# A hybrid attention and state-space block: the state-space loads in another order, and its prelude in buffers of its own

## The chip, the cores and the metric

The kernel runs on one core of one Trainium2 chip. TensorE (PE), VectorE (DVE), ScalarE (ACT), GpSimd (POOL) and SyncE (SP) each work through a list of instructions of their own, in order; DMA transfers are issued from queues, nearly all of them from SP's. The metric is the device time of one execution in microseconds (us).

## The reference, cut to what matters

One layer over 512 tokens of width 1024, float32. One projection feeds three token mixers: DSA (attention over keys that an indexer picks), NSA (compressed, selected and windowed attention) and SSD (a state-space mixer, 32 heads in 4 groups, 4 chunks of 128 tokens). Their outputs are projected, gated, summed, projected again, and a feed-forward network follows. The change concerns the SSD mixer:

```python
dtc = softplus(dt + dt_bias)                 # a step per token and head
a = -exp(a_log)
a_cum = cumsum(dtc * a, axis=2)              # along the 128 tokens of a chunk
lmat = exp(where(tril, a_cum_i - a_cum_j, -inf))
cb = einsum('bcign,bcjgn->bcijg', cm, bm)
y_diag = einsum('bcijg,bcijgh,bcjgh,bcjghp->bcighp', cb, lmat, dtc, xs)
states = einsum('bcjgn,bcjgh,bcjghp->bcghpn', bm, exp(a_cum[:, :, -1:] - a_cum) * dtc, xs)
h_in = scan over chunks: h = h * exp(a_cum[:, :, -1]) + states
y_off = einsum('bcign,bcghpn,bcigh->bcighp', cm, h_in, exp(a_cum))
y = rms_norm((y_diag + y_off + xs * d_skip) * silu(z), norm_g)
```

## The kernel before, in words

Two streams of work are written out together. The **filler** is the stream of projections: matmuls into PSUM tiles `pj`, three per product (high and low halves of both operands: lines 359 to 361), with weight blocks loaded by SP (`wraw`), split by ACT (`whi`, line 158) and DVE (`wlo`, line 159). The **main** stream runs the DSA indexer (a top-k by repeated `max` and `match_replace` on DVE, lines 766 to 774), the SSD prelude, the DSA attention of 16 units, the SSD mixer of 16 units, and the NSA attention. Generators yield amounts of work, and a scheduler with a timeline of its own then fixes each engine's order; the chip runs that order as it stands.

PSUM has two buffers for `pj`, two for `sc`, two for `pT`, one each for `pv` and `pF`. A pool tag `gt` with two SBUF buffers (`TG` is 2) holds, in turn, outputs that go to memory. The z projections use it:

```python
def cbz(t, p):
    zo = gp.tile([128, 512], F32, name="zo", tag="gt", bufs=TG)
    act.activation(zo, p, AF.Tanh, scale=0.5)
    dve.scalar_tensor_tensor(zo, zo, 1.0, p, op0=ALU.add, op1=ALU.mult)
    nc.sync.dma_start(zs_d[...], zo)
```

A `pj` buffer is free again when DVE has done the second of these (line 619). The two tiles `pre` of the SSD prelude come from the same tag: from the prelude's first operation until its last tile has gone to `ac_d` in memory, they are the two `gt` buffers.

The SSD mixer works on 16 units (a group and a chunk each; units 0, 1, 2, ... alternate between two groups). A unit loads `E` (the row of `a_cum` spread over partitions, 512 KB), `xs` and `zs` (256 KB each) and `bcx` (B transposed, B and C, three loads of 64 KB), all on SP's queue. `stage2` makes the product of C and B on PE (line 1139, "cb"), a mask on POOL (line 1142), eight exponentials on ACT (1145) and a product on DVE (1152), all in `E`; `stage3` makes the unit's output from `E` and `xt` with eight matmuls on PE (line 1180, "py"), the state's matmuls before them (1163, 1170), then two DVE operations and a transpose (1191). Each of the four tiles has two buffers, and the loads of unit i+2 are written ahead of `stage3` of unit i, which is the last to read the buffers that they go to.

Of the kernel before, what the change touches and what calls it, by code (L numbers as in the profile page):

```python
# [7 lines left out]
F32 = mybir.dt.float32  # L8
# [26 lines left out]
R0, R1, R2, R3 = 1000.0, 1.5, 2.5, 0.5  # L35


def build_kernel(ctx, tc, A, out):
    nc = tc.nc
# [14 lines left out]
    def popen(name, side="left", space=None, bufs=1):  # L54
        kw = dict(name=name, bufs=bufs, side=side)
        if space is not None:
            kw["space"] = space
            kw.pop("side")
        cm = tc.tile_pool(**kw)
        p = cm.__enter__()  # L60
        open_pools[name] = cm
        return p

    def pclose(name):
        open_pools.pop(name).__exit__(None, None, None)
# [8 lines left out]
    xs_d = scratch("xs_d", [S, 2048])  # L74
    bt_d = scratch("bt_d", [S, 512])
# [13 lines left out]
    def ps(tag, shape, dt=F32, bufs=2):  # L89
        if tag == XT[0]:  # L90
            XT[1] += 1
            if XT[1] % 3 == 0:
                tag = "pF"
        return psp.tile(shape, dt, tag=tag, name=tag, bufs=PSB[tag])
# [7 lines left out]
    gp = popen("gt")  # L102
# [757 lines left out]
    def pipeline(units, ratio):  # L860
        prev = None
        for u in units + [None]:
            if u is not None:
                if u.load is not None:
                    yield from u.load()
                u.prep()
                yield from a1(u, ratio)
            if prev is not None:
                yield from b1(prev, ratio)
            if u is not None:  # L870
                a2(u)
            prev = u
# [182 lines left out]

    def ssd_prelude():
        n = [128, 128]
        pre = [gp.tile([128, 4, 128], F32, name="pre", tag="gt", bufs=TG) for _ in range(2)]
        t = {k: pre[i // 4][:, i % 4] for i, k in enumerate("xaebsuvt")}
        tri1 = t["t"]  # L1060
        pool.memset(tri1, 1.0)
# [25 lines left out]
        dta = t["e"]  # L1087
        dve.scalar_tensor_tensor(dt3(dta), dt3(dt), -1.0, bc(av[:, None, :], [128, 4, 32]), op0=ALU.mult, op1=ALU.mult)
        yield 700.0
        ones = t["u"]  # L1090
        pool.memset(ones, 1.0)
        p = ps("pT", [128, 512])
# [9 lines left out]
        dve.tensor_scalar(sv["ea"], sv["ea"], 0.5, None, op0=ALU.mult)  # L1102
        dve.tensor_scalar(dskip, dskip, 0.5, None, op0=ALU.mult)
        yield 700.0
        p = ps("pT", [128, 512])
        pe.transpose(p[:, 0:128], sv["acm"], ident)
        at_ = t["s"]
        dve.tensor_copy(at_, p[:, 0:128])
        nc.sync.dma_start(ac_d, at_)
        return sv  # L1110

    def ssd(sv, ratio):
        sp = popen("ssd", side="right")
# [4 lines left out]
        def stage1(g, c):  # L1118
            u = U()
            u.g, u.c = g, c  # L1120
            rows = slice(c * 128, c * 128 + 128)
            cols = slice(g * 512, g * 512 + 512)
            u.E = sp.tile([128, 8, 128], F32, name="E", bufs=2)
            nc.sync.dma_start(u.E, bcast_rows(ac_d, c * 32 + g * 8, 8))
            u.xs = sp.tile([128, 512], F32, name="xs", bufs=2)
            nc.sync.dma_start(u.xs, xs_d[rows, cols])
            u.zs = sp.tile([128, 512], F32, name="zs", bufs=2)
            nc.sync.dma_start(u.zs, zs_d[rows, cols])
            u.b = sp.tile([128, 3, 128], F32, name="bcx", bufs=2)
            nc.sync.dma_start(u.b[:, 0], bt_d[rows, g * 128:g * 128 + 128])  # L1130
            nc.sync.dma_start(u.b[:, 1], BC_d[g * 128:g * 128 + 128, rows])
            nc.sync.dma_start(u.b[:, 2], BC_d[512 + g * 128:512 + g * 128 + 128, rows])
            return u

        def stage2(u):
            g, c = u.g, u.c
# [65 lines left out]
        def need(i):  # L1202
            if i < 16:
                g, c = order[i]
                if c == 0:
                    yield f"x{g}"
                    yield f"z{g}"
                us.append(stage1(g, c))
        us = []
        yield from need(0)  # L1210
        yield from need(1)
        yield from stage2(us[0])
        for i in range(16):
            yield from need(i + 2)
            if i + 1 < 16:
                yield from stage2(us[i + 1])
            if TR:
                TR.pop()()
                yield ratio * 436
            yield from stage3(us[i])  # L1220
        TR.pop()()
        yield ratio * 436
        sst = sp.tile([128, 4], F32, name="sst")
# [12 lines left out]
    def bcast_rows(t, r0, n):  # L1236
        a = t[r0:r0 + n, :]
        return bass.AP(tensor=a.tensor, offset=a.offset, ap=[[0, 128]] + [list(e) for e in a.ap])
# [240 lines left out]
    def main():  # L1479
        nonlocal at  # L1480
        HI[0] = 0
        yield from dsa_index(mk)
        yield "dq"
        yield "nkv"
        sv = yield from ssd_prelude()
        at = popen("att", side="right")
        HI[0] = HM
        yield from pipeline(dsa_units(), R1)
        pclose("att")
        pclose("mask")  # L1490
        yield from ssd(sv, R3)
        XT[0] = "pT"
        yield "nq"
        at = popen("att", side="right")
        yield from pipeline(nsa_units(R2), R2)
        done.add("nsa")
        yield "c1"
        pclose("att")
        pclose("kv")
# [60 lines left out]
```

## Time and profile before

| | us |
|---|---|
| median of three runs | 1436.81 (1435.62 to 1438.63) |
| the profiled execution, its own time | 1434.21 |
| span from the first to the last instruction in it | 1432.5 |
| PE busy in it | 1364.9 |
| from the first cb (404.5) to the end of the SSD's last transposes (about 591) | 187 |

The profiled execution stands 2.6 us below the median of the runs. Its own time is 1.7 us more than its span. PE's busy time counts matmuls that overlap once; what PE lacks to the span is idle time.

### The profile page before, as it was taken

The numbers are of one execution on the slowest core, as the hardware profiler recorded it, in microseconds if no ns is written. First come the engines' busy times: TensorE is split into PE (matmuls) and PEld (weight loads), VectorE is DVE, ScalarE is ACT, GpSimd is POOL, SyncE is SP. The second block draws the span as 40 slices with busy tenths as digits, with TensorE's granted clock in tenths as the row PEclk, the third lists the DMA queues.
The fourth block names the chain that finished last, engine by engine and source line by source line (L and its number), as shares of the span: only waits on it lengthen the run. The fifth ranks groups of instructions, "written<-read, shape, count | busy, mean of one in ns | idle before, by whom it ended". The sixth has DMA issues, their size and how long they took to land.

```text
span 1432.5 us, 19782 instructions
## 1 busy us (share of the span) xinstructions
PE 1364.9 (95%) x6736; PEld 1121.9 (78%) x6736; DVE 1089.1 (76%) x1944; ACT 722.5 (50%) x1442; POOL 482.4 (34%) x342
## 2 busy tenths in 40 slices
PE   6989799999999989999999999999799999999988
PEld 5878688888887767888888777787589888888866
DVE  4599966898977555488568897888655797979796
ACT  5545236667665675555555555545324444444442
POOL 5455211101056676111013524424000342526265
PEclk9999899999999999999999999999899999999999
DMA  6336464453586688843337743424555232331401
GB/s 202 81 96 139 126 205 126 136 133 103 139 229 200 202 230 218 229 141 107 89 94 208 207 129 100 117 65 131 178 184 172 79 118 89 106 115 53 136 4 59
DMA packets 232098, 195.93 MB, mean 137 GB/s; under 512 B 17200, under 2 KB 183484, under 8 KB 231996
## 3 DMA queue, kind: packets, MB, share of 16 engines
q1 hardware_dynamic: 226524, 183.12, 44.3%
q0 software_dynamic: 4608, 8.39, 2.2%
q10 hardware_dynamic: 864, 3.15, 0.6%
q8 instruction: 53, 0.87, 0.3%
q14 instruction: 49, 0.40, 0.1%
HBM read 157.85 MB, written 36.77 MB: 136 GB/s over the span
## 4 chain that ended last, share of the span: by engine, by line
PE 70%; DVE 14%; DMA 7%; issue 4%; ACT 3%; POOL 2%; SPq 1%; DVEq 0%; POOLq 0%; ACTq 0%
PE pj L359 16%; PE pj L360 16%; PE pj L361 15%; PE sc L359 3%; PE sc L361 3%; PE sc L360 3%; PE pT L831 2%; DVE wlo L159 2%; PE sc L796 2%; PE sc L795 2%; PE pv L844 2%; PE pv L843 1%; DMA gld<-g_d 1%; DVE mask L766 1%; DMA E<-ac_d 1%
## 5 line engine op out<-in xcount | busy, mean ns | idle before, releaser
L158 ACT ACTIVATE whi<-wraw 128x1024 fp32r<-128x1024 f32 (+3 forms) x180 | 173.2, 971 | 176.3 <-PE pj L360 115.7
L159 DVE TENSOR_TENSOR wlo<-wraw,whi 128x1024 fp32r<-128x1024 f32 (+1 forms) x156 | 192.9, 1238 | 60.3 <-ACT whi L158 59.2
L359 PE MATMUL pj<-hTh,whi 128*128 128x512 f32 x384 | 154.9, 403 | 0.4 <-DVE cacc L726 0.4
L361 PE MATMUL pj<-hTh,wlo 128*128 128x512 f32 x384 | 153.6, 400 | 0.0
L360 PE MATMUL pj<-hTl,whi 128*128 128x512 f32 x384 | 153.3, 399 | 0.0
L359 PE MATMUL pj<-whi,hTh 128*128 128x512 f32 (+2 forms) x352 | 141.6, 404 | 8.3 <-DVE stk L429 3.1
L804 ACT ACTIVATE p<-p,nb,rs 128x256 f32<-128x256 f32 (+3 forms) x192 | 123.2, 645 | 52.0 <-DVE nb L802 52.0
L360 PE MATMUL pj<-wlo,hTh 128*128 128x512 f32 (+2 forms) x352 | 139.6, 397 | 0.1
L361 PE MATMUL pj<-whi,hTl 128*128 128x512 f32 (+2 forms) x352 | 138.3, 393 | 0.0
L159 DVE TENSOR_TENSOR wlo<-qd,whi 128x1024 fp32r<-128x1024 f32 x56 | 101.3, 1815 | 25.6 <-ACT whi L158 25.6
L359 PE MATMUL pj<-yh,whi 128*128 128x512 f32 x256 | 103.6, 409 | 9.8 <-ACT yh L709 8.2
L815 POOL TENSOR_TENSOR p<-p,rc 128x256 f32<-128x256 f32 (+3 forms) x48 | 38.2, 796 | 220.7 <-DVE rc L810 67.1
L158 ACT ACTIVATE whi<-qd 128x1024 fp32r<-128x1024 f32 x56 | 58.9, 1055 | 87.6 <-PE sc L361 38.9
L360 PE MATMUL pj<-yl,whi 128*128 128x512 f32 x256 | 102.6, 401 | 0.3 <-DVE yl L710 0.3
L361 PE MATMUL pj<-yh,wlo 128*128 128x512 f32 x256 | 102.3, 400 | 0.0
L359 PE MATMUL sc<-whi,fh 128*128 128x512 f32 x224 | 88.9, 397 | 8.2 <-DVE u2acc L1460 4.8
L360 PE MATMUL pj<-h2l,whi 128*128 128x512 f32 (+1 forms) x256 | 96.3, 376 | 0.0
L361 PE MATMUL pj<-h2h,wlo 128*128 128x512 f32 (+1 forms) x256 | 96.2, 376 | 0.0
L359 PE MATMUL pj<-h2h,whi 128*128 128x512 f32 (+1 forms) x256 | 96.1, 376 | 0.0
L360 PE MATMUL sc<-wlo,fh 128*128 128x512 f32 x224 | 88.6, 396 | 0.0
L361 PE MATMUL sc<-whi,fo 128*128 128x512 f32 x224 | 88.3, 395 | 0.0
L359 PEld LDWEIGHTS pj<-whi,hTh 128*128 128x128 f32 x352 | 68.2, 194 | 22.4 <-issue 6.6
(349 smaller groups left out, 3476.3 us busy)
## 6 DMA issues: line engine op xcount, KB each, us to landing
wraw<-in_w_in_dram SPq DMA_DIRECT2D x84, 512.0 KB, 4.4
wraw<-in_w_ff_dram SPq DMA_DIRECT2D x32, 512.0 KB, 4.3
qd<-in_w_ff_dram SPq DMA_DIRECT2D x32, 512.0 KB, 4.7
gld<-g_d SPq DMA_DIRECT2D x48, 256.0 KB, 3.2
q_d<-qev SPq DMA_DIRECT2D x128, 64.0 KB, 2.7
qu<-q_d POOLq DMA_DIRECT2D x32, 256.0 KB, 3.6
E<-ac_d SPq DMA_DIRECT2D x16, 512.0 KB, 4.9
wraw<-in_w_br_ssd_dram SPq DMA_DIRECT2D x16, 512.0 KB, 4.0
```

Source lines behind the costliest of these rows:

```text
L158: act.activation(hi[:, :m], r[:, :m], AF.Copy)
L159: (pool if i < NP else dve).tensor_tensor(lo[:, :m], r[:, :m], f(hi[:, :m]), op=ALU.subtract)
L359: pe.matmul(o, lh, rh, start=first, stop=False)
L360: pe.matmul(o, lh, rl, start=False, stop=False)
L361: pe.matmul(o, ll, rh, start=False, stop=last)
L766: dve.scalar_tensor_tensor(wk, r[:, :n], iwt[:, b, h:h + 1], caus[:, 384 - 128 * b:] if h == 0 else wk, op0=ALU.mult, op1=ALU.add)
L795: pe.matmul(s_[:, h % w, :n], u.q[:, h], kh[:, :n], start=True, stop=False)
L796: pe.matmul(s_[:, h % w, :n], u.q[:, h], kl[:, :n], start=False, stop=True)
L804: act.activation(u.p[h][:, :n], u.p[h][:, :n], AF.Exp, bias=u.nb[:, h:h + 1], scale=rs8[:, u.b, u.h0 + h:u.h0 + h + 1], accum_out=u.sm[:, ...
L815: pool.tensor_tensor(u.p[h][:, :n], u.p[h][:, :n], bc(rc[:, h:h + 1], [128, n]), op=ALU.mult)
L831: pe.transpose(pt[:, h], u.p[h][:, kb * 128:kb * 128 + 128], ident)
L844: pe.matmul(o, vk, pl0, start=False, stop=en)
```

## The change

The prelude gets a pool of its own, `pre`, on the side of SBUF where the indexer's tiles lay, closed after the DSA attention. Its last two parts (the matmuls with what reads them, and the transpose with the store to `ac_d`) become generators of their own and run as the `load` of units 5 and 7 of the DSA attention. In the SSD mixer `bcx` and `xs` have three buffers, the loads of `bcx` stand first, `E` of unit i+2 is loaded after `stage3` of unit i, and `zs` of unit i+1 just before its `stage2`.

```diff
--- before.py
+++ after.py
@@ -1055,7 +1055,8 @@
 
     def ssd_prelude():
         n = [128, 128]
-        pre = [gp.tile([128, 4, 128], F32, name="pre", tag="gt", bufs=TG) for _ in range(2)]
+        pp_ = popen("pre", side="right")
+        pre = [pp_.tile([128, 4, 128], F32, name="pre", bufs=2) for _ in range(2)]
         t = {k: pre[i // 4][:, i % 4] for i, k in enumerate("xaebsuvt")}
         tri1 = t["t"]
         pool.memset(tri1, 1.0)
@@ -1087,6 +1088,9 @@
         dta = t["e"]
         dve.scalar_tensor_tensor(dt3(dta), dt3(dt), -1.0, bc(av[:, None, :], [128, 4, 32]), op0=ALU.mult, op1=ALU.mult)
         yield 700.0
+        return sv, t, tri1, dta
+
+    def ssd_prelude2(sv, t, tri1, dta):
         ones = t["u"]
         pool.memset(ones, 1.0)
         p = ps("pT", [128, 512])
@@ -1102,12 +1106,14 @@
         dve.tensor_scalar(sv["ea"], sv["ea"], 0.5, None, op0=ALU.mult)
         dve.tensor_scalar(dskip, dskip, 0.5, None, op0=ALU.mult)
         yield 700.0
+
+    def ssd_prelude3(sv, t):
         p = ps("pT", [128, 512])
         pe.transpose(p[:, 0:128], sv["acm"], ident)
         at_ = t["s"]
         dve.tensor_copy(at_, p[:, 0:128])
         nc.sync.dma_start(ac_d, at_)
-        return sv
+        yield 100.0
 
     def ssd(sv, ratio):
         sp = popen("ssd", side="right")
@@ -1120,17 +1126,21 @@
             u.g, u.c = g, c
             rows = slice(c * 128, c * 128 + 128)
             cols = slice(g * 512, g * 512 + 512)
-            u.E = sp.tile([128, 8, 128], F32, name="E", bufs=2)
-            nc.sync.dma_start(u.E, bcast_rows(ac_d, c * 32 + g * 8, 8))
-            u.xs = sp.tile([128, 512], F32, name="xs", bufs=2)
-            nc.sync.dma_start(u.xs, xs_d[rows, cols])
-            u.zs = sp.tile([128, 512], F32, name="zs", bufs=2)
-            nc.sync.dma_start(u.zs, zs_d[rows, cols])
-            u.b = sp.tile([128, 3, 128], F32, name="bcx", bufs=2)
-            nc.sync.dma_start(u.b[:, 0], bt_d[rows, g * 128:g * 128 + 128])
+            u.b = sp.tile([128, 3, 128], F32, name="bcx", bufs=3)
             nc.sync.dma_start(u.b[:, 1], BC_d[g * 128:g * 128 + 128, rows])
             nc.sync.dma_start(u.b[:, 2], BC_d[512 + g * 128:512 + g * 128 + 128, rows])
+            nc.sync.dma_start(u.b[:, 0], bt_d[rows, g * 128:g * 128 + 128])
+            u.xs = sp.tile([128, 512], F32, name="xs", bufs=3)
+            nc.sync.dma_start(u.xs, xs_d[rows, cols])
             return u
+
+        def load_E(u):
+            u.E = sp.tile([128, 8, 128], F32, name="E", bufs=2)
+            nc.sync.dma_start(u.E, bcast_rows(ac_d, u.c * 32 + u.g * 8, 8))
+
+        def load_z(u):
+            u.zs = sp.tile([128, 512], F32, name="zs", bufs=2)
+            nc.sync.dma_start(u.zs, zs_d[u.c * 128:u.c * 128 + 128, u.g * 512:u.g * 512 + 512])
 
         def stage2(u):
             g, c = u.g, u.c
@@ -1208,16 +1218,22 @@
                 us.append(stage1(g, c))
         us = []
         yield from need(0)
+        load_E(us[0])
         yield from need(1)
+        load_E(us[1])
+        load_z(us[0])
         yield from stage2(us[0])
         for i in range(16):
             yield from need(i + 2)
             if i + 1 < 16:
+                load_z(us[i + 1])
                 yield from stage2(us[i + 1])
             if TR:
                 TR.pop()()
                 yield ratio * 436
             yield from stage3(us[i])
+            if i + 2 < 16:
+                load_E(us[i + 2])
         TR.pop()()
         yield ratio * 436
         sst = sp.tile([128, 4], F32, name="sst")
@@ -1482,11 +1498,15 @@
         yield from dsa_index(mk)
         yield "dq"
         yield "nkv"
-        sv = yield from ssd_prelude()
+        sv, *rest = yield from ssd_prelude()
         at = popen("att", side="right")
         HI[0] = HM
-        yield from pipeline(dsa_units(), R1)
+        us = dsa_units()
+        us[5].load = lambda: ssd_prelude2(sv, *rest)
+        us[7].load = lambda: ssd_prelude3(sv, rest[0])
+        yield from pipeline(us, R1)
         pclose("att")
+        pclose("pre")
         pclose("mask")
         yield from ssd(sv, R3)
         XT[0] = "pT"
```

The scheduler then orders every engine anew. Up to the prelude's matmuls PE's order is the same; behind them, as far as the last projections of the branches, pieces of attention, mixer and filler stand at other places against each other. Three places follow, with the rows of each engine's order.

PE, before, in the middle of the first z projection (`pj`), where the prelude's two cumulative sums (lines 1093, 1094) and its transpose (1106) stand:

```order
L360 MATMUL pj<-wlo,hTh 128x512
L361 MATMUL pj<-whi,hTl 128x512
L1093 MATMUL pT<-pre 128x128
L1094 MATMUL pT<-pre 128x128
L1106 MATMUL pT<-ident,sv_acm 128x128
L359 MATMUL pj<-whi,hTh 128x512
L360 MATMUL pj<-wlo,hTh 128x512
```

PE, after: at the old place there are only matmuls of `pj`; the two sums (now lines 1097 and 1098) stand in the DSA attention, between the value matmuls of a unit (843, 844) and the next unit's transposes (831), and the transpose (now 1112) 124 rows further on.

```order
L844 MATMUL pv<-ptl,v_d 128x512
L843 MATMUL pv<-pth,v_d 128x512
L1097 MATMUL pT<-pre 128x128
L1098 MATMUL pT<-pre 128x128
L359 MATMUL pj<-hTh,whi 128x512
L360 MATMUL pj<-hTl,whi 128x512
L844 MATMUL pv<-ptl,v_d 128x512
L831 MATMUL pT<-ident,p 128x128 x4
L361 MATMUL pj<-hTh,wlo 128x512
```

So three matmuls have moved from the top-k's time into that of the attention, some 425 rows of PE's order later.

DVE, before, at the same place: the prelude's readers of those sums, between steps of the top-k on the mask of the last query block (771, 772), and behind them the first two outputs of the z projection (619).

```order
L1095 COPY sv_acm<-pT 128x128
L1096 TENSOR_SCALAR sv_nac<-pT 128x128
L771 MAX m_1603<-mask_1326 128x8
L1108 COPY pre<-pT 128x128
L1102 TENSOR_SCALAR sv_ea<-sv_ea 128x128
L1098 TENSOR_TENSOR pre<-pT,sv_acm 128x128
L772 MATCH_REPLACE mask_1326<-m_1603,mask_1326 128x512
L1100 SCALAR_TENSOR_TENSOR sv_dw<-sv_dw,sv_dth 128x128
L771 MAX m_1622<-mask_1326 128x8
L619 SCALAR_TENSOR_TENSOR zo<-zo,pj 128x512
L772 MATCH_REPLACE mask_1326<-m_1622,mask_1326 128x512
L619 SCALAR_TENSOR_TENSOR zo<-zo,pj 128x512
```

DVE, after, around the last `vz` operations: the readers are gone, and an output (619) stands ahead of these rows, one within them and one at their end, with three steps of the top-k between the last two.

```order
L513 TENSOR_TENSOR qev<-pF,qev 128x512
L584 TENSOR_TENSOR vz<-pT,vz 32x64 x4
L772 MATCH_REPLACE mask_1326<-m_1544,mask_1326 128x512
L771 MAX m_1594<-mask_1326 128x8
L619 SCALAR_TENSOR_TENSOR zo<-zo,pj 128x512
L772 MATCH_REPLACE mask_1326<-m_1594,mask_1326 128x512
L771 MAX m_1603<-mask_1326 128x8
L772 MATCH_REPLACE mask_1326<-m_1603,mask_1326 128x512
L771 MAX m_1622<-mask_1326 128x8
L772 MATCH_REPLACE mask_1326<-m_1622,mask_1326 128x512
L771 MAX m_1625<-mask_1326 128x8
L619 SCALAR_TENSOR_TENSOR zo<-zo,pj 128x512
```

The prelude's own 19 DVE operations (lines 1064 to 1088 before, done early in the kernel) now begin behind the last step of the top-k (774), between the first operations of the DSA attention.

SP's queue, before, in the middle of the SSD mixer: from the load of `E` of unit 5 to that of unit 6. The `bcx` loads are those of unit 5, `xs` is unit 6's, `zs` is unit 5's, `yc_d` the store of unit 2; the numbers tell buffers apart.

```order
L1124 DMA E_4269<-ac_d_96 128x1024
L1128 DMA zs_4273<-zs_d_94 128x512
L142 DMA wraw_5094<-in_w_in_dram 128x2x512
L1195 DMA yc_d_97<-yev_4305 128x4x128
L1126 DMA xs_4348<-xs_d_91 128x512
L1130 DMA bcx_4275<-bt_d_92 128x128
L1131 DMA bcx_4275<-BC_d_93 128x128
L1132 DMA bcx_4275<-BC_d_93 128x128
L744 DMA xs_d_91<-xev_4948 128x4x128
L142 DMA wraw_5161<-in_w_in_dram 128x2x512
L1124 DMA E_4346<-ac_d_96 128x1024
```

After, from the load of `zs` of unit 4 on: `bcx` of unit 5 (4271) and `E` of unit 5 (4346), and at once `bcx` of unit 6 (4348), which before stood behind `E` of unit 6.

```order
L1143 DMA zs_4277<-zs_d_94 128x512
L1134 DMA xs_4352<-xs_d_91 128x512
L1130 DMA bcx_4271<-BC_d_93 128x128
L1131 DMA bcx_4271<-BC_d_93 128x128
L1132 DMA bcx_4271<-bt_d_92 128x128
L142 DMA wraw_5156<-in_w_in_dram 128x2x512
L744 DMA xs_d_91<-xev_4950 128x4x128
L1139 DMA E_4346<-ac_d_96 128x1024
L1205 DMA yc_d_97<-yev_4305 128x4x128
L1130 DMA bcx_4348<-BC_d_93 128x128
L1131 DMA bcx_4348<-BC_d_93 128x128
L1132 DMA bcx_4348<-bt_d_92 128x128
```

So each `bcx` load has moved forward by about one unit against the loads of `E`.

## Rows read from the trace of the kernel before

**Rows 1.** The page: busy time by engine; busy tenths in 40 slices.
```profile
PE 1364.9 (95%) x6736; PEld 1121.9 (78%) x6736; DVE 1089.1 (76%) x1944; ACT 722.5 (50%) x1442; POOL 482.4 (34%) x342
...
PE   6989799999999989999999999999799999999988
```

**Rows 2.** PE's longest wait, 130 to 190 us: total, times, longest.
```profile
PE pT L1106 <- DVE sv_acm L1095: 3.1, 1, 3.1
```

**Rows 3.** PE in order of time, 156 to 182 us: start, duration, idle before.
```profile
159.33 0.39 PE L361 MATMUL pj<-whi,hTl 128*128 128x512 f32 x1
161.10 0.46 PE L1093 MATMUL pT<-pre 128*128 128x128 f32 x2 [1.39 <-DVE vz L584]
...
168.28 0.79 PE L359 MATMUL pj<-whi,hTh 128*128 128x512 f32 x1 [2.90 <-DVE zo L619]
...
172.66 0.39 PE L360 MATMUL pj<-wlo,hTh 128*128 128x512 f32 x1
172.89 0.40 PE L361 MATMUL pj<-whi,hTl 128*128 128x512 f32 x1
```

**Rows 4.** Busy times of PE, PEld, DVE, ACT, POOL; clock; DMA share; GB/s.
```profile
164.00:168.00 4.00, 0.47 (x1) 0.18 (x1) 3.97 (x12) 2.06 (x5) 0.00 (x0) 0.50 0.41 85
```

**Rows 5.** DVE in order of time, 156 to 200 us.
```profile
156.37 0.69 DVE L771 MAX8 m<-mask 128x8 f32<-128x512 f32 x1
156.99 1.21 DVE L159 TENSOR_TENSOR wlo<-wraw,whi 128x1024 fp32r<-128x1024 f32 x1
...
167.56 0.67 DVE L619 SCALAR_TENSOR_TENSOR zo<-zo,pj 128x512 f32<-128x512 f32 x1
...
188.60 0.42 DVE L774 TENSOR_SCALAR mask<-mask 128x512 f32<-128x512 f32 x1
193.02 0.69 DVE L619 SCALAR_TENSOR_TENSOR zo<-zo,pj 128x512 f32<-128x512 f32 x1 [4.00 <-ACT zo L618]
```

**Rows 6.** DVE, 44 to 58 us: first and last of the prelude's 19.
```profile
46.51 1.13 DVE L1064 TENSOR_TENSOR pre<-dtr,dtb 128x128 f32<-128x128 f32 x1
...
56.87 0.28 DVE L1088 SCALAR_TENSOR_TENSOR pre<-pre,av 128x128 f32<-128x128 f32 x1
```

**Rows 7.** PE's longest wait in total, 404 to 591 us.
```profile
PE pT L1139 <- DMA bcx<-BC_d: 6.0, 4, 3.2
```

**Rows 8.** PE in order of time, 517 to 531 us.
```profile
523.26 0.46 PE L1139 MATMUL pT<-bcx 128*128 128x128 f32 x2 [3.24 <-DMA bcx<-BC_d]
...
528.55 0.40 PE L360 MATMUL pj<-wlo,hTh 128*128 128x512 f32 x1
```

**Rows 9.** SP's queue in order of time, 396 to 600 us.
```profile
494.51 0.32 SPq L1124 DMA_DIRECT2D E<-ac_d  x1
...
519.58 0.43 SPq L1132 DMA_DIRECT2D bcx<-BC_d  x1
```

**Rows 10.** PE in order of time: unit 7's last py, unit 9's first.
```profile
492.32 1.00 PE L1180 MATMUL sc<-xt,E 128*128 128x64 f32 x8
...
506.36 1.55 PE L1180 MATMUL sc<-xt,E 128*128 128x64 f32 x12 [0.49 <-DVE E L1152]
```

**Rows 11.** SSD mixer, and from there to 1008 us; columns as in rows 4.
```profile
404.00:591.00 187.00, 177.38 (x924) 141.11 (x925) 121.49 (x145) 117.89 (x311) 113.62 (x86) 0.99 0.78 218
591.00:1008.00 417.00, 405.13 (x2055) 331.78 (x2054) 327.13 (x786) 222.46 (x491) 125.86 (x109) 1.00 0.45 131
```

**Rows 12.** POOL on tile E and on xs, durations in ns (min, median, max).
```profile
L1142 POOL TENSOR_SCALAR_AFFINE_SELECT E<-E x16: 1083/1093/2086, 401.8 to 572.0; 128x1024 f32<-128x1024 f32 x16
L1147 POOL TENSOR_TENSOR xt<-xs,sv_dth x16: 1035/1044/2026, 402.9 to 568.2; 128x512 f32<-128x512 f32 x16
```

**Rows 13.** Loads of E, from issue to landing.
```profile
DMA to landing us min/median/max: 3.9/4.9/5.8
```

**Rows 14.** Loads of bcx, from issue to landing.
```profile
DMA to landing us min/median/max: 1.9/3.4/5.6
```

**Rows 15.** PE in order of time, 1000 to 1050 us.
```profile
1016.45 1.22 PE L359 MATMUL pj<-yh,whi 128*128 128x512 f32 x2 [7.17 <-ACT yh L709]
```

## The prediction

> **What bounds the kernel now.** I read the page first. PE is busy for 1364.9 of 1432.5 us, and in most of the 40 slices it has nothing left to give [rows 1]. A change that adds no matmul and takes none away can only win or lose in the 67.6 us in which PE stands idle, and in stretches where it runs at the lower of its two clocks. So the question of every part is: which of PE's waits ends, and does another take its place?
>
> The table of waits shows two clusters in the part that the change touches. The first lies at 159 to 172 us, where the prelude's three matmuls stand in PE's order. PE waits 1.4 us in front of the first sum [rows 3], 3.1 us for the copy of its result, `sv_acm` [rows 2], and 2.9 us for an output of the z projection, `zo` [rows 3]. PE's own timeline gives what it costs in all [rows 3]: the last `pj` matmul before starts at 159.33, the next ones at 168.28, ten of these run slowly, and the eleventh starts at 172.66. The slowness is the clock: 0.50 granted from 164 to 168 us, 1.2 instead of 2.4 GHz [rows 4]. From 172.66 on matmuls start 0.23 us apart again, as at full clock [rows 3]. What PE did ahead of the fall is plain, too: nearly nothing from 160 us on.
>
> Why does PE stand still there? Each of the three waits ends in DVE, and DVE is not slow in one operation, it is full: 3.97 of 4 us between 164 and 168 [rows 4]. It works through the top-k, and the prelude's readers queue in that. The output `zo` came last, at 167.56 [rows 5], since its buffer was one of the two that the prelude held until `ac_d` was stored. So the prelude holds up PE twice, by its own matmuls and by its buffers.
>
> The second cluster is the SSD mixer, 404 to 591 us. PE is busy for 177.4 of 187 us [rows 11], and 6.0 of the missing 9.6 us are four waits of a unit's first product for its `bcx` loads [rows 7]. The longest, 3.24 us, ends at 523.26; the third `bcx` load was issued at 519.58 [rows 8, 9]. A `bcx` buffer is free only when the unit two before has done its state's matmuls, and the load then queues behind others. This wait, too, is followed by slow matmuls, up to 528.55 [rows 8].
>
> **Part one, the prelude.** At full clock `pj` matmuls start every 0.23 us [rows 3]. Without prelude, waits and slow clock, the eleventh would start at 159.33 + 11 x 0.23 = 161.9 instead of 172.66: 10.8 us are freed. The three moved matmuls are pairs of passes, of which the first took 0.46 us with the wait of one pass for the other [rows 3]; back to back I take 0.27, so 0.8 us is paid again in the attention. That leaves 10.0.
>
> Does a new wait come? DVE stays as full: the top-k ends at 189 us before [rows 5], and afterwards it can hardly end earlier. I walked DVE's new order with the durations of the trace from 158.8 us on (0.7 us a `max` or `match_replace`, 1.2 a `wlo`, 0.67 a `zo`) [rows 5]. The first four `zo` end at 159.5, 164.9, 169.9 and 177.1; PE, which makes a tile in 24 matmuls or 5.45 us, wants their buffers at 159.7, 165.2, 170.6 and 176.1. Only the fourth is late, by 1.0 us. The next ones are early by 1 us and more. **Part one: -9.0 us**, with bounds of 10.0 (no `zo` late) and 5 (a second `zo` late by as much as the old one, 2.9 us, and 1.5 us of slow matmuls behind it, as at 523 us, below).
>
> The prelude's own 19 DVE operations took 46.51 to 57.15 before [rows 6], where PE wasn't waiting; moving them away from there wins nothing. They now stand behind 188.6. Their cover is DVE's idle time there, 4.0 us in front of a single operation [rows 5], and, beyond that, the time in which PE has `pj` matmuls to do. Without that cover the first attention units would come up to 10.6 us later, the whole stretch of 46.51 to 57.15, which costs PE nothing while the filler has matmuls: PE was full from 180 to 396 us [rows 1]. The sums and the transpose in the attention hold one `pT` buffer each for a few DVE operations; nothing but later work reads their results. The two DVE readers block no `zo` by more than 0.6 us. I take zero for all this.
>
> **Part two, the loads.** With three buffers and ahead of `E`, a `bcx` load waits for the unit three before. I went through SP's new order with PE's: each `bcx` load can go out 6 to 20 us before its product is due on PE, and such a load lands in 5.6 us at most [rows 14]. So the 6.0 us go [rows 7], and with the longest of them the slow stretch behind it: 523.26 to 528.55 holds seven `pj` and about 2.1 us of other matmuls, 3.7 us at full clock, so 1.5 us are freed [rows 8]. Together -7.5.
>
> What is late next is `E`. Its buffers stay two, and its load now stands behind `stage3`. Unit 9 shows how long the way from a py to the py two units on is: unit 7's last ends at 493.3, `E` is issued at 494.51, and unit 9's first py starts at 506.36 after a wait for DVE's product in `E` [rows 9, 10]: 13.0 us. In the new order the mixer is denser: 361 instead of 475 `pj` matmuls stand between the first cb and the last transposes. The work on PE between unit i-2's last py and unit i's first, counted at full clock, is 14 to 22 us for most units, 13.3 for unit 2, and only 11.5 for unit 8 (29 `pj`, eight py, 13 transposes, one state product, two cb). So unit 8 waits 1.5 us. **Part two: -6.0 us**, with bounds of -9.6 (all waits of the mixer gone, [rows 11], and no new one) and +2.3 (below).
>
> On a rule of the Trainium skill: its page "DMA: Bandwidth & Descriptors", section "Latency and other measured facts", puts the HBM's access latency at 0.2 us on average and 2 us at high load. By that an estimate for the denser mixer is 1.8 us more on `E`'s way, and part two would come to about -2 instead of -6; the trace's loads of `E` spread over less than 2 us at a DMA share of 0.78 [rows 11, 13], so I stay with the row.
>
> **The sum.** -9.0 - 6.0 = -15.0 us against the profiled execution's 1434.2: 1419.2. The median of the runs lies 2.6 above that execution, so for the median 1436.8 - 15 = 1421.8, rounded **1422**. Behind the mixer PE's work is unchanged, and the order of the last attention rows against the filler is, too: the 7.17 us wait at 1016 stays [rows 15].
>
> **The rivals.** *`E` is late, the loads win nothing.* If `E` takes its longest landing, 5.8 instead of 4.9 [rows 13], and POOL its long mask, 2.09 instead of 1.09 [rows 12], the way is 13.0 + 0.9 + 1.0 = 14.9 us, and 16 if DVE's product in `E` is slowed by a like amount. Then units 2, 6, 7, 8, 9 and 15 wait, by 2.7, 1.4, 1.4, 4.5, 1.9 and 1.5: 13 us, less some that one wait saves the next; I take 10. Part two becomes +2.3, the sum -6.7: 1430. For it: the mixer runs on less filler. Against it: units 10 to 14 show no such wait now. *The gain is given back.* From 591 to 1008 us PE stands idle for 11.9 us already [rows 11], and an order made anew may double that: -3 to 0 in all, 1435. Against it: the NSA attention begins 57 `pj` matmuls earlier in the new order and ends at the same place, so it is looser. *POOL becomes the pace, and the kernel slower.* POOL is busy for 113.6 us of the mixer's 187 [rows 11]; the new order has some 152 us of PE work there. The same POOL operation takes 1.04 us or, while DVE is at work, up to 2.03 [rows 12]. The mixer has 16 masks and 64 products or sums of that size on POOL, 84 us at their shortest and 163 at their longest; of the 30 us that the 113.6 exceed the 84 by I count half as other work. That is up to 178 us, 26 more than PE, so +11 in all: 1448. It turns from a gain to a loss where POOL's sum passes 152 + 15 = 167. Against it: now the sum is 1.35 times the shortest at most, and would have to be 1.8 times. The Trainium skill has the rule in "GPSIMD Engine Reference", section "Key points": GpSimd shares its SBUF interfaces with VectorE; the trace's two durations agree. *More is won.* If half to two thirds of those 11.9 us go as well, since the NSA attention begins earlier, and no `zo` is late: -22 to -24, 1414.
>
> **How the numbers follow.** Forecast 0.62, by itself 1416 to 1427. `E` late 0.14, given back 0.10, POOL's pace 0.04, more won 0.10. The range leaves out the upper half of "given back", POOL's pace and a part of "more won": 1414 to 1434. A measurement of this kernel tells about 0.2%, 2.9 us, from no change. Faster takes forecast, `E` late and more won, 0.86; same 0.08, most of "given back"; slower 0.06, the rest of that and POOL's pace.
>
> **What the profile after would show.** Part one is right if PE has no wait over 1 us and a granted clock of 1.00 from 156 to 190 us, and the first attention product (line 795 as before) starts near 194 us with some 37 more `pj` matmuls done. Part two is right if the wait for `BC_d` at the first product is gone, and waits of py for `E` sum to under 3 us. A sum of over 8 us there, or a POOL busier than 85% of the mixer, is the first or third rival. If both parts hold and the time doesn't fall by 10 us, the loss lies between 600 and 1010 us. What would make the prediction wrong is a place in the new order where PE, in order as it is, meets an operation whose input the scheduler's timeline thought ready.

## The result: slower, by 0.6%

The changed kernel takes 1444.39 us (median of seven runs, 1441.27 to 1448.95), the kernel before 1438.56 (seven runs, 1432.21 to 1441.98): a ratio on record of 1.0061, interval 1.0043 to 1.0080 (the two medians alone are 0.4% apart, 5.8 us). 1422 was forecast, 1414 to 1434 the range; the prediction is wrong, in its sign too.

The profiled execution took 1445.04 us, its span 1443.3. That is 10.8 us over the span of the profiled execution before, about twice the distance of the medians, so what follows accounts for two single executions. From the page: busy time, and PE's busy tenths and granted clock in 40 slices [rows 1].

```profile
PE 1374.3 (95%) x6736; PEld 1128.1 (78%) x6736; DVE 1089.8 (76%) x1944; ACT 721.1 (50%) x1442; POOL 487.7 (34%) x342
...
PE   6989999999999989899999999899699999999987
...
PEclk9999999999999999999999999999799999999999
```

With the same 6736 matmuls PE is busy 9.4 us longer, and its idle time is 69.0 us (67.6 before): no idle time was won, and more matmuls ran slowly. The mean granted clock of the two executions is 0.987 before and 0.982 of full after.

First what held. The window in which the prelude stood, then PE's waits in 156 to 200 us [rows 2 to 4]:

```profile
156.00:190.00 34.00, 33.47 (x147) 26.80 (x147) 32.93 (x67) 10.83 (x20) 0.00 (x0) 1.00 0.63 187
```
```profile
PE pj L359 <- DVE zo L619: 0.5, 1, 0.5
```

PE is full, at full clock (1.00), with one wait of 0.5 us left of the old three. The mixer's waits, PE, 408 to 580 us (line numbers there are 10 higher than before: py is 1190, the first product 1149) [rows 7]:

```profile
PE sc L1190 <- DVE E L1162: 3.5, 4, 1.3
PE pT L1201 <- DVE hst L1186: 2.0, 2, 1.4
PE pF L509 <- DVE qev L513: 1.6, 1, 1.6
PE pT L1180 <- ACT cbm L1151: 1.2, 1, 1.2
...
PE pT L1149 <- DMA bcx<-BC_d: 0.3, 1, 0.3
```

The wait for `BC_d` is gone, 6.0 to 0.3 us. In its place stand longer waits for what the engines make in a unit. Only the first is for an input, the product in `E` (0.5 us before). In the next three, by the code, PE waits for a PSUM buffer, `pT` or `pF`, until the operation named has read it: the one that adds up the state `hst` (no such wait before), the split `qev` (0.4 before), and the copy `cbm` (1.1 before). So the loads no longer hold PE up, and the mixer's idle time stays: 170 - 158.6 = 11.4 us, by the second of the next rows, against 190 - 180.4 = 9.6 before. They are the DSA attention, the mixer, and the rest up to the projection of the mixed outputs [rows 11]; columns as in rows 4. The mixer's last transpose starts at 593.9 us in the kernel before, not at about 591 as given ahead of the prediction, so the mixer is cut there.

```profile
196.00:408.00 212.00, 210.85 (x1067) 176.02 (x1067) 176.05 (x393) 134.44 (x271) 20.01 (x29) 1.00 0.50 136
408.00:578.00 170.00, 158.57 (x829) 123.73 (x828) 112.50 (x131) 107.31 (x297) 121.01 (x88) 0.98 0.75 216
578.00:1052.00 474.00, 448.18 (x2192) 365.45 (x2191) 348.14 (x817) 240.09 (x516) 126.19 (x109) 0.97 0.46 135
```

The same two stretches, mixer and rest, before:

```profile
404.00:594.00 190.00, 180.38 (x940) 143.59 (x940) 122.28 (x147) 118.27 (x311) 114.64 (x87) 0.99 0.78 217
594.00:1040.00 446.00, 426.07 (x2127) 347.17 (x2126) 345.56 (x810) 234.19 (x506) 124.85 (x108) 0.99 0.45 133
```

Behind the mixer PE stands idle for 474 - 448.2 = 25.8 us, against 19.9 before. Two places show how. PE in order of time where the NSA attention begins, and where its last product with V ends and the projection of its output begins [rows 15]:

```profile
596.16 1.03 PE L916 MATMUL sc<-kc,qu 128*128 128x64 f32 x4 [2.82 <-issue]
597.00 0.77 PE L795 MATMUL sc<-kh_w,qu 128*128 128x512 f32 x1
597.57 0.63 PE L796 MATMUL sc<-kl_w,qu 128*128 128x512 f32 x1
```
```profile
1019.82 0.49 PE L844 MATMUL pv<-ptl,v_s 128*128 128x512 f32 x1
1027.53 1.22 PE L359 MATMUL pj<-yh,whi 128*128 128x512 f32 x2 [7.21 <-ACT yh L709]
1028.55 0.63 PE L360 MATMUL pj<-yl,whi 128*128 128x512 f32 x1
...
1032.36 0.40 PE L361 MATMUL pj<-yh,wlo 128*128 128x512 f32 x1
```

After each wait matmuls take 0.63 instead of 0.40 us: the granted clock is at half, 1.2 GHz.

The first place is new. In the kernel before PE went from filler to that product at 606.01 us without a wait. After the change PE waits 1.7 us for the mixer's last scale (`rst`) and then the 2.82 us; the load of the product's `qu`, the first of four in the second line, landed at 595.96:

```profile
PE pT L1245 <- POOL rst L1243: 1.7, 1, 1.7
591.94 2.23 POOL L876 DMA_DIRECT2D qu<-q_d  x4 [11.44 <-ACT gth L677]
```

The second place was there before as well, with 7.17 us. These 7.21 us are a way through memory, in the timeline of all engines:

```profile
1021.69 0.58 SPq L852 DMA_DIRECT2D yb_d<-yt  x1
...
1024.19 0.80 SPq L708 DMA_DIRECT2D yr<-yb_d  x2
...
1026.85 1.26 ACT L709 ACTIVATE yh<-yr 128x512 fp32r<-128x512 f32 x2 [5.90 <-DMA yr<-yb_d]
```

The store goes out at 1021.69, the load of the same rows can go out 2.50 us later and is there 2.66 us after that. The Trainium skill, "DMA: Bandwidth & Descriptors", section "Latency and other measured facts", gives a DMA a fixed cost of some 2 us, most of it the round trip to the target memory; two in a row would be some 4 us by that, an estimate, and the trace has 5.2.

**An account of the span.** The 2976 projection matmuls up to the mixed outputs are the filler, 0.227 us each. What a stretch lasts beyond its filler is main work, waits and slow clock together. Stretches are cut at matmul starts in the timeline, the filler is counted in PE's order. Each cell: length, filler count, rest.

| stretch, up to | before | after | rest, after - before | forecast |
|---|---|---|---|---|
| first DSA product | 195.4, 638, 50.5 | 195.8, 676, 42.4 | -8.1 | -9.0 |
| first cb | 209.1, 634, 65.2 | 212.7, 644, 66.5 | +1.3 | 0 |
| mixer's last transpose | 189.4, 475, 81.6 | 168.7, 361, 86.7 | +5.1 | -6.0 |
| first mixed-output product | 446.4, 1229, 167.4 | 474.3, 1295, 180.4 | +13.0 | 0 |
| end | 392.2 | 391.8 | -0.4 | 0 |

The sum is +10.9, the spans differ by 10.8. (Of the filler, 192 matmuls with fewer columns stand in the first stretch; they are the same in both kernels.) The first attention product starts when it did before:

```profile
195.37 0.40 PE L795 MATMUL sc<-kh_d,qu 128*128 128x256 f32 x2
195.81 0.40 PE L795 MATMUL sc<-kh_d,qu 128*128 128x256 f32 x2
```

PE stands in no wait there, it comes from filler. But the product couldn't have come much sooner: it reads `qu`, whose load goes out 0.6 to 0.8 us behind the last `match_replace` of the top-k in all the kernels of this text, at 188.74 before and 191.07 after, and landed at 194.1 and 194.2. In two of the kernels below (loads alone with R1 0.7; the kernel before with R2 2.0) the product starts 0.04 us after its load landed. So the end of the top-k on DVE sets this place, and the filler done by then is what PE had time for. What the prelude freed is 38 projections done earlier, and what the mixer freed is 114 moved out of it. The end came no sooner for either.

A single execution's stretch isn't sharp: loads alone, below, has the order of the kernel before on PE up to the mixer, yet its first product starts at 199.4.

### The profile page after: what moved, and what is told of

Read it like the earlier page. It is cut to its first block, busy times and chain, and to the rows that moved or that the text cites. A ratio compares the mean times of both kernels' runs of the same rounds, so it can differ in the third digit from the quotient of the medians.

```text
span 1443.3 us, 19789 instructions
## 1 busy us (share of the span) xinstructions
PE 1374.3 (95%) x6736; PEld 1128.1 (78%) x6736; DVE 1089.8 (76%) x1944; ACT 721.1 (50%) x1442; POOL 487.7 (34%) x342
## 4 chain that ended last, share of the span: by engine, by line
PE 61%; DVE 15%; DMA 8%; issue 6%; ACT 5%; POOL 3%; SPq 1%; DVEq 0%; ACTq 0%; POOLq 0%
PE pj L359 14%; PE pj L360 14%; PE pj L361 14%; PE sc L359 3%; PE sc L360 3%; PE sc L361 3%; DVE wlo L159 3%; PE pT L831 2%; ACT p L804 2%; DMA E<-ac_d 2%; DMA gld<-g_d 2%; PE sc L796 1%; PE sc L795 1%; PE pv L844 1%; PE pv L843 1%
## 5 line engine op out<-in xcount | busy, mean ns | idle before, releaser
L158 ACT ACTIVATE whi<-wraw 128x1024 fp32r<-128x1024 f32 (+3 forms) x180 | 173.2, 971 | 183.8 <-PE pj L360 112.4
L159 DVE TENSOR_TENSOR wlo<-wraw,whi 128x1024 fp32r<-128x1024 f32 (+1 forms) x156 | 198.2, 1273 | 54.0 <-ACT whi L158 52.2
L359 PEld LDWEIGHTS pj<-hTh,whi 128*128 128x128 f32 x384 | 72.7, 189 | 16.5 <-DVE cacc L726 1.8
```

Source lines behind the costliest of these rows:

```text
L158: act.activation(hi[:, :m], r[:, :m], AF.Copy)
L159: (pool if i < NP else dve).tensor_tensor(lo[:, :m], r[:, :m], f(hi[:, :m]), op=ALU.subtract)
L359: pe.matmul(o, lh, rh, start=first, stop=False)
```

## The experiments

Ratios are to the kernel before, timed on the same chip in the same session (its medians there: 1433.0 to 1435.1 us).

**The parts alone.** Theory 1 then was: the prelude wins, the load part loses. Theory 2: the prelude's gain is given back, the loads are worth nothing.

```diff
 prelude alone: the change without its part in ssd()
 loads alone:   the change in ssd() only
 buffers alone: ssd_prelude() whole, as before, but
-        pre = [gp.tile(..., tag="gt", bufs=TG) ...]
+        pp_ = popen("pre", side="right")
+        pre = [pp_.tile(..., bufs=2) ...]
 E early: the changed kernel, in stage1 behind the load of xs
+            load_E(u)
+            load_z(u)
```

Prelude alone: 

> The prelude part alone, with the state-space loads as they were before. Theory 1 (the prelude part wins about what was forecast, the load part loses more): 7 to 9 us under the kernel before, 1430 for a kernel before of 1438. Theory 2 (the prelude's gain is given back by whatever stands behind it, and the loads are worth nothing): within 3 us of the kernel before.

 Measured: 1.0098 (1.0077 to 1.0120).

Loads alone: 

> The load part alone, with the prelude as it was before. In its order 389 projection matmuls stand between the first and the last matmul group of the state-space units, against 475 before. Theory 1: 10 to 16 us above the kernel before, about 1451, with no wait of TensorE for BC_d and instead waits for E, yv and the work behind the state-space stretch. Theory 2: within 3 us of the kernel before.

 Measured: 1.0017 (1.0002 to 1.0032).

Buffers alone: 

> Own buffers for the prelude, its matmuls left where they stand in the text, loads as before. Theory 1 with the buffers as the cause of the prelude's gain: within 3 us of the kernel with the prelude part alone, about 1430, since the shared buffers held up the gates and with them the projections. If the moving of the matmuls is the cause: within 3 us of the kernel before.

 Measured: 1.0092 (1.0069 to 1.0115).

E early: 

> The changed kernel with the loads of E and zs put back behind the small ones of the same unit (three buffers stay); TensorE's order is the same as in the changed kernel, row by row. If the late load of E is what costs: 4 to 8 us under the changed kernel, and the waits of py for E below 1 us in total. If the thinner filler costs (theory 1): within 3 us of the changed kernel.

 Measured: 1.0046 (1.0028 to 1.0064); py's waits for `E` are 3.5 us as in the changed kernel. (In PE's order one first product stands four matmuls later.)

Theory 1 fell: the prelude part, which wins its time where it should (rest of the first stretch 40.2 and 38.6 us, against 50.5), is the one that loses by itself. That the late load of `E` costs anything isn't seen: 1.0046 lies within 3 us of the changed kernel, and the waits for `E` are as long. Where does the prelude alone lose? From its trace, PE by line between 990.6 and 1024.5 us:

```profile
L831 PE MATMUL pT<-ident,p 128*128 128x128 f32 x20 | 4.9, 318 | 1.4 <-DVE p L817 1.4
L831 PE MATMUL pF<-ident,p 128*128 128x128 f32 x12 | 3.4, 335 | 0.7 <-DVE p L817 0.7
L983 PE MATMUL pv<-cph,vz 128*128 128x128 f32 x12 | 3.3, 426 | 1.4 <-DVE yt L851 1.4
L844 PE MATMUL pv<-ptl,v_s 128*128 128x512 f32 x6 | 3.2, 541 | 1.0 <-DVE ptl L836 0.9
L843 PE MATMUL pv<-pth,v_s 128*128 128x512 f32 x6 | 3.0, 506 | 0.7 <-ACT pth L835 0.7
```

No `pj` is among the lines: the attention ends bare. The filler is used up at 990.1 us but for the last 96 matmuls, which stand behind the last `pv` in this order, and the window shows the stretch:

```profile
990.00:1025.00 35.00, 23.84 (x102) 17.69 (x100) 22.78 (x88) 20.60 (x62) 4.99 (x8) 0.75 0.24 72
```

PE is idle for 11.2 of 35 us, at a clock of 0.75. Buffers alone has such a bare stretch of 20.6 us. Hence theory B: from the top-k on the main stream and its engines set the time, the filler covers PE's waits, and a projection done early is missing as cover later. Theory A is the prediction's: PE's work sets the time.

**Less and more filler.** The kernel before, in five tiles of the z projection:

```diff
-        pe.matmul(o, ll, rh, start=False, stop=last)
+        for j in range(npass - 2):   # npass 2 (fewer) or 4 (more)
+            pe.matmul(o, ll, rh, start=False, stop=last and j == npass - 3)
```

Fewer: 

> The kernel before with 40 filler matmuls left out (the third pass of five tiles of the z projection, so the low half of the activations is missing there): 40 x 0.227 = 9.1 us less work for TensorE, early in the program. Theory A (TensorE's work sets the time): 9 us faster. Theory B (the main stream, from the top-k on, sets the time, and the filler only covers its waits; what is done of it or saved early is missing as cover at the end of the NSA attention): no faster than by 3 us, perhaps slower, with a stretch of over 15 us without a projection matmul before the last pv, as in the kernel with the prelude part alone (34.7 us).

 Measured: 1.0012 (0.9995 to 1.0028), with a bare stretch of 19.1 us at 998.

More: 

> The kernel before with the same 40 filler matmuls done twice (the low half of the activations counts twice in five tiles of the z projection): 9.1 us more work for TensorE. Theory A: 9 us slower. Theory B: less than 5 us slower.

 Measured: 1.0126 (1.0101 to 1.0151), 18 us.

Taking 9.1 us of work from PE wins nothing, where theory A expected 9 us. In the profiled execution PE is busy for 1363.0 us, only 1.9 less than before, and idle for 72.3 (67.6): 7.2 us came back as slower matmuls and 4.7 as idle time. By stretch the rest grew by 5.7 us up to the first attention product, 4.1 in the mixer and 2.3 behind it, so mostly ahead of the end that theory B named. And the scheduler sorted this kernel anew too; by the next runs re-sorting alone is worth more than 9 us, so one such kernel is evidence against theory A, but not proof. Adding 9.1 us costs twice as much, which neither theory expected. The profiled execution is 22.7 us longer: 9.1 are the added work, 3.5 more idle time (71.1), and the other 10.1 the same matmuls running slower. The mean granted clock over all runs is 0.980 with more filler, 0.980 with less, and 0.985 in the kernel before, so the lower clock isn't the added work's.

**The same work in another order.** The paces (R1 for DSA, R2 for NSA, R3 for the mixer) only say how much filler is written out beside a unit of main work; each number below leaves the instructions as they are and makes the scheduler sort them anew.

```diff
-R0, R1, R2, R3 = 1000.0, 1.5, 2.5, 0.5
+R0, R1, R2, R3 = 1000.0, <R1>, <R2>, <R3>
```

Changed kernel, R3 1.0: 

> The changed kernel with the pace of the state-space units against the filler at 1.0 instead of 0.5: TensorE's order is the same up to the mixer, and 168 instead of 97 projection matmuls then stand behind the NSA attention's last score matmul. Theory B: the 7.2 us wait for yh behind the last pv goes and the clock holds there, 7 to 10 us under the changed kernel, so at or under the kernel before. If the order of the filler doesn't matter: within 3 us of the changed kernel, 1.004 to 1.008 of the kernel before.

 Measured: 0.9979 (0.9960 to 0.9999).

Changed kernel, R1 0.7: 

> The changed kernel with the pace of the DSA units against the filler at 0.7 instead of 1.5: 361 projection matmuls in the mixer as in the changed kernel, 168 instead of 97 behind the last score matmul. Theory B: as the run before, 7 to 10 us under the changed kernel. Order doesn't matter: within 3 us of it.

 Measured: 0.9935 (0.9909 to 0.9961).

Changed kernel, R1 0.7 and R3 1.0: 

> The changed kernel with both paces altered (DSA units 0.7, state-space units 1.0). The mixer holds 354 projection matmuls, as in the run with 0.7 alone (360), but 96 instead of 168 stand behind the last score matmul, as in the changed kernel (97). Theory B (filler kept for the end of the NSA attention is what made the run with 0.7 fast): the wait for yh of some 7 us comes back and the time is 7 to 10 us above that run, about the kernel before. Otherwise, if the rest of the order made it fast: within 3 us of that run, 0.992 to 0.996 of the kernel before.

 Measured: 1.0043 (1.0025 to 1.0060), the wait for `yh` 7.0 us.

Prelude alone, R1 0.5 and R2 2.0: 

> The prelude part alone, with paces (DSA 0.5, NSA 2.0) that leave projection matmuls up to the last pv (108 behind the last score matmul; none between the last score matmuls and the end with the prelude part alone as it was). Theory B: the bare stretch at the end cost the prelude part its gain, so now 3 to 9 us under the kernel before. If the prelude in its own buffers costs by itself: over 5 us above the kernel before again.

 Measured: 1.0007 (0.9991 to 1.0022).

Kernel before, R1 0.7: 

> The kernel before with the DSA pace at 0.7: a control. 96 instead of 115 projection matmuls behind the last score matmul, the mixer as before (477). Theory B: the pace alone wins nothing, within 4 us of the kernel before, rather above. If the pace is what made the other run fast: 6 us or more under it.

 Measured: 1.0116 (1.0095 to 1.0138).

Loads alone, R1 0.7: 

> The load part alone with the DSA pace at 0.7; 396 projection matmuls in the mixer, 146 behind the last score matmul, the prelude as before with its waits at 160 us. Against the run with both parts and 0.7 it lacks only the prelude part. Theory B: that part is worth its 9 us where the end isn't bare, so this run stands within 3 us of the kernel before. If the prelude part is worth nothing: as fast as that run, 0.991 to 0.996 of the kernel before.

 Measured: 1.0068 (1.0046 to 1.0090).

The first three moved the way theory B said, the second and third by some 15 to 18 us instead of 7 to 10: R1 0.7 beats both kernels. The other three missed: the prelude alone gets its 0.9% back in an order whose end isn't bare, but wins nothing over that; the two last lose more than expected. So four more. PE's order in the first three is that of a kernel already timed (R1 0.7, R1 0.7, and before) up to the mixer's end and for some 140 to 150 projections behind it:

Changed kernel, R1 0.7, R2 1.5: 

> The changed kernel with paces 0.7 for DSA and 1.5 instead of 2.5 for NSA: up to the end of the mixer the order is that of the run with 0.7 alone; 96 instead of 168 projection matmuls stand behind the last score matmul, 94 instead of 113 behind the last pv, and 15 instead of 59 among the last 24 matmuls of the attention. Theory B: the wait of 7 us for yh is back, and 8 to 15 us are lost against that run, 1.002 to 1.006 of the kernel before. If there is no such rule: 0.991 to 0.997.

 Measured: 1.0030 (1.0009 to 1.0051); 12.1 us without a projection and 4.4 us of waits for `yh` in place of the one wait of 7.

Changed kernel, R1 0.7, R2 2.0: 

> The same with an NSA pace of 2.0: 172 projection matmuls behind the last score matmul, 120 behind the last pv. Theory B: no wait for yh over 4 us, as fast as the run with 0.7 alone, 0.990 to 0.997 of the kernel before. No rule: anything from 0.993 to 1.006.

 Measured: 0.9996 (0.9982 to 1.0011).

Kernel before, R2 2.0: 

> The kernel before with an NSA pace of 2.0 instead of 2.5: up to the end of the mixer the order of the kernel before; 96 instead of 115 projection matmuls behind the last score matmul, 15 instead of 48 among the last 24 matmuls of the attention. Theory B: slower, 1.003 to 1.012. No rule: within 0.3% on either side.

 Measured: 1.0067 (1.0042 to 1.0091).

Changed kernel, R1 1.8: 

> The changed kernel with a DSA pace of 1.8 instead of 1.5: 349 projection matmuls in the mixer (361), 178 behind the last score matmul (97), 120 behind the last pv (84). Theory B: 0.990 to 0.999 of the kernel before, with no wait for yh over 4 us. No rule: about the changed kernel, 1.003 to 1.008.

 Measured: 0.9924 (0.9900 to 0.9949).

The last is the fastest of all: 1424.63 us, 10.5 under the kernel before. PE where its NSA attention ends:

```profile
995.58 0.40 PE L361 MATMUL pj<-yh,wlo 128*128 128x512 f32 x1
995.81 0.40 PE L844 MATMUL pv<-ptl,v_s 128*128 128x512 f32 x1
996.55 0.50 PE L359 MATMUL pj<-yh,whi 128*128 128x512 f32 x1 [0.35 <-DVE gld L1339]
996.89 0.40 PE L360 MATMUL pj<-yl,whi 128*128 128x512 f32 x1
...
1001.67 0.39 PE L360 MATMUL pj<-yl,whi 128*128 128x512 f32 x1
```
```profile
978.00:1030.00 52.00, 45.91 (x198) 35.35 (x197) 36.65 (x61) 23.26 (x45) 15.37 (x12) 1.00 0.61 197
```

Projections of outputs that are long there run on behind the last `pv` while the last output goes through memory, and the clock holds at 1.00, where the changed kernel stood for 7.21 us and then ran at half.

R2 2.0 with R1 0.7 is the miss of this group. It has no wait for `yh` (0.8 us), but one at the attention's start, for a load whose data went through memory too:

```profile
594.68 1.03 PE L916 MATMUL sc<-kc,qu 128*128 128x64 f32 x4 [4.42 <-DMA qu<-q_d]
595.52 0.77 PE L795 MATMUL sc<-kh_w,qu 128*128 128x512 f32 x1
596.10 0.63 PE L796 MATMUL sc<-kl_w,qu 128*128 128x512 f32 x1
```

PE's order up to there is that of R1 0.7, where the same product waited for 1.2 us. So this wait isn't the order's, and it doesn't settle why the run missed.

**All kernels with the same matmuls**, by the filler left behind the last `pv`; rest as in the table above, from one profiled execution each (these stand up to 5 us from their medians).

| behind the last pv | kernels | rest behind the mixer | ratio |
|---|---|---|---|
| 108 to 132 | R1 1.8; loads alone; R1 0.7; R1 0.7 R2 2.0; R3 1.0 | 156.6, 159.5, 160.0, 169.5, 171.8 | 0.9924, 1.0017, 0.9935, 0.9996, 0.9979 |
| 84 to 99 | before; loads R1 0.7; R1 0.7 R3 1.0; prelude R1 0.5 R2 2.0; R1 0.7 R2 1.5; before R2 2.0; E early; before R1 0.7; changed | 167.4, 164.7, 171.1, 172.8, 173.2, 174.2, 176.5, 176.5, 180.4 | 1, 1.0068, 1.0043, 1.0007, 1.0030, 1.0067, 1.0046, 1.0116, 1.0061 |
| 96, end bare | buffers alone; prelude alone | 175.1, 181.2 | 1.0092, 1.0098 |

The first group's mean rest is 163.5 us, the second's 173.0. Within a group some 15 us are left that this count doesn't order, and by their ratios the groups overlap (loads alone stands above the kernel before). The count stands in the expectations of three of the last four runs; the other kernels are sorted by it afterwards. Before and changed have the same count, 84, so it doesn't explain the 13.0 us between these two.

## Why the prediction was wrong

**Part one held in its place.** -9.0 was forecast up to the first attention product, -8.1 came; in the eleven kernels with all matmuls and the prelude's own buffers the rest of that stretch is 38.6 to 43.7 us, in the five with the shared ones 49.9 to 54.6. Full clock, one wait of 0.5 us, and 38 more projections done, as stated.

**The step that failed is the sum.** It took what PE was freed of at 160 us from the end of the program. That presumes that PE's work is the chain. The prediction had the opposite in hand: the top-k would hardly end earlier, and the first attention product would start near 194 us with 37 more projections done. So the gain was filler done ahead of time. It reaches the end only if the stretches behind become shorter by as much, and they didn't: with 38 projections less to do, their rest grew by 19.0 us, 13.9 of them outside the mixer. The prelude alone, with the loads as before, shows it without part two: against the kernel before its rest is -10.3 us up to the first attention product, and then +3.1, +5.2 and +13.7 in the next three stretches. The run with 9.1 us less filler agrees, in the one order in which it was made. That the missing cover is what made the rest grow is theory B, argued and not shown for the changed kernel.

**"Behind the mixer PE's work is unchanged" failed by 13.0 us.** What was read off the order was right for the very end: 84 projections stand behind the last `pv` in both kernels, and the wait of 7.17 us stayed, at 7.21. But behind the last score matmul there are 97 instead of 115. PE's idle time rose from 446 - 426.1 = 19.9 to 25.8 us, by 5.9: 4.5 at the attention's start, the two new waits there, and 1.4 in the last 44 us.

The other 7.1 us are slower matmuls: PE is 22.1 us longer busy, and 66 more projections are 15.0 of that. Most of these lie behind the new waits at the start (half clock from 595.4 to 602.2 us) and around the last `pv` (0.81 granted in 1008 to 1052, where it was 0.88 in 996 to 1040). So over half of the 13.0 us came up at the start of the attention, which the prediction took to be looser, since it begins 57 projections earlier. Its sign for a loss, the stretch between 600 and 1010 us, points beside the place: idle time is 9.5 us in 597 to 1008 and was 9.5 in 606 to 996. The prediction had this as "the gain is given back", at a chance of 0.10 and with at most 11.9 us. As a size that is about what came behind the mixer, but half of it was clock, which the rival didn't count; and since part two lost as well, the kernel ended above the rival's -3 to 0.

**Part two was mis-sized, +5.1 instead of -6.0.** The removed wait went as said. The forecast gave unit 8 a new wait of 1.5 us; there came four waits for `E`, 3.5 us, and 4.8 us for PSUM buffers, against 0.5 and 1.5 by the same operations before. Those for `E` aren't the load's: with `E` loaded early they are the same. It is tempting to put the longer rest down to the thinner cover (361 instead of 475 projections between the same main work), but the runs don't bear that out: with the old loads and 481 and 506 projections buffers alone and prelude alone have a rest of 91.7 and 86.8 us, loads alone with 389 has 93.1, and R3 1.0 with only 342 has 83.1. So what made the mixer's rest grow stays open. POOL was busy for 121.0 of 170 us, 71%; the rival of POOL's pace didn't come. In the rival on a late `E` a sum is off by a little: -7.5 + 10 is +2.5, not +2.3.

**What the change is worth** can't be told from one order of it. Seven sortings of the changed kernel's instructions span 0.9924 to 1.0061; three of the kernel before 1 to 1.0116. The paces 1.5, 2.5 and 0.5 give the best of the three and the worst of the seven. Two kernels alike up to the mixer's end, the kernel before and R2 2.0 on it, differ by 0.67%: as much as the change.

What stays open: why the mixer's rest grew, what orders the rests within a group of the last table, and why added filler costs its time twice.

## What to carry to other kernels

Before a freed wait is subtracted from the end, ask whether the next thing on the critical stream starts earlier; if it waits for another engine, as here for the top-k, the gain is only filler done early, and one must look for the place where that filler will be missing. Look at the places where a result goes through memory and back, here the start and the end of the last attention, and keep independent work for them: in R1 1.8 that took away the wait and the half clock at the end. A change to a kernel whose order a scheduler makes, with pace numbers written by hand, is judged only over several of them: re-sorting alone moved this one by 1.4%.

## What the runs showed of the hardware

A long wait of PE costs twice, but the second part is smaller than the time at half clock. In the changed kernel the clock was granted at half from 1022.1 to 1032.3 us, 10.2 us around the end of the 7.21 us wait; but PE was busy for only 4.8 of them, in which eleven matmuls started 0.43 us apart instead of 0.23. So the wait cost about 2.4 us more, an estimate from these times. Over the whole execution the clock was at half for 52.6 us, in which PE was busy for 41.5 (37.9 and 27.4 before); a mean granted clock doesn't tell the two apart.

The lower clock doesn't follow the amount of work: the mean over the runs is 0.980 with 9.1 us more filler and with 9.1 us less, and 0.985 in the kernel before.

PE waits that look alike aren't: one product of the same PE order waited for 1.2 us in one profiled execution and for 4.4 in another.
